# Three of an expert's 24 weight residuals move from VectorE to GpSimd in a two-layer encoder kernel

## The chip, the cores and the metric

The kernel runs on one core of a Trainium2 chip as one launch. The metric is the device time of that launch in microseconds (us), and lower is better. Engines are named as in the profile: PE is TensorE's matmul, PEld its weight load, DVE is VectorE, ACT is ScalarE, POOL is GpSimd, SP is SyncE, whose queue issues the weight loads.

## The reference

Two identical layers work on 512 tokens of width 1024 in float32. Each has a mixer (a state-space scan, a stick-breaking attention and a retention, gated and projected) and a mixture of experts. Only the latter is touched. Every token goes to two of 16 experts, and an expert has three 1024x1024 weights:

```python
def expert_block(args):
    xb, e = args
    hb = jax.nn.silu(xb @ w1[e]) * (xb @ w3[e])
    return hb @ w2[e]
```

The results are weighted by the router's gates and added up for each token.

## The kernel before

**Precision by splitting.** A float32 product is made of three matmuls in fp32r. Each operand is split into a rounded part and the rest: for a weight, ACT copies the raw tile into `wh` (fp32r), and then DVE computes `wl = raw - wh`. `mm3` multiplies with high times high, high times low and low times high. The two lines that matter:

```python
        with self.tc.high_priority(0 if self.calm else self.ahead):
            self.cut = (nc.scalar.copy(hv, v).ins,
                        (eng or nc.vector).tensor_tensor(lv, v, hv.bitcast(F32), OP.subtract).ins)
```

`wh` is line L342 in the profile and `wl` is L343. The argument `eng` of `split_half` chooses the engine of the residual; without it that is DVE.

**The experts.** A weight is loaded as four transfers of 1 MB (`raw`, 128 partitions x 2048), and each transfer holds two k-tiles of 128x1024. So an expert has 24 k-tiles: k = 0 to 7 for each of W1, W3 and W2. For one k-tile PE runs six matmuls of 512 columns (`mm3` for n = 0 and n = 1): L348 with `wh`, L349 with `wl`, L350 with `wh` again. L349 is the first that needs `wl`. The tokens of an expert lie in 96 slots (`CAP`).

**Buffers.** The pool `split` has four `wh` and four `wl`. So ACT can write the `wh` of a k-tile only when PE is through with the k-tile four before it. Raw tiles have some ten buffers of 1 MB in several pools, taken in a fixed order (`ORDER`).

**Order.** The loop over e in `moe` issues W1 of expert e (`expert_in`), then W2 of expert e-1 (`expert_out`), the transposes of the tokens of e+1 (`tx`, with `hx` written by ACT and DVE, L1266 and L1267), the gather of the tokens of e+2 (`fetch`, L1182, an indirect DMA that POOL issues), W3 of e, and then `expert_mid`: `sl = silu(a1) * a3` (ACT L1291, DVE L1292), its transposes (L1264) and their split (`gh`, `gl`, L1266 and L1267). The output `y` of W2 is scaled by the gate on ACT (L1313) and stored from ACT's queue. Each engine runs its own queue in order. A planner writes these queues out at build time, from the priorities given in the code and from costs that it assumes; the splits get a lead of 200 places (`AHEAD`).

**POOL in the experts' stage.** It issues the gathers. In layer 0, from expert 4 (`PREP`) on, it also computes the parameters of layer 1's state-space scan (`s5_params`), in pieces that the generator `step()` lets go, two an expert, until the generator is done and `prep` is None again. In layer 1 there is no next layer, and POOL has the gathers alone. POOL computes the residuals of expert 0's first four k-tiles in either layer, and some of the mixer's.

Of the kernel before, what the change touches and what calls it, by code (L numbers as in the profile page):

```python
# [25 lines left out]
NE = 16  # L26
# [12 lines left out]
PREP = 4  # L39
# [84 lines left out]
class Kernel:  # L124
# [1147 lines left out]
    def expert_in(self, w, x, mkload, tag, ready=()):  # L1272
        ps = [self.bank(t, "e13")[0:CAP] for t in tag]
        for u in range(4):
            if 2 * u >= len(ready):
                v = mkload(w, u)
            for kk in range(2):
                k = 2 * u + kk
                h, lo = ready[k] if k < len(ready) else self.split_half(v[:, kk:kk + 1, :], (1, 1024))
                for n in range(2):  # L1280
                    ns = slice(n * 512, (n + 1) * 512)
                    self.mm3(ps[n], x[0][k], x[1][k], h[:, 0, ns], lo[:, 0, ns], k == 0, k == 7)
        return ps

    def expert_mid(self, pool, a1, a3):
        nc = self.nc
        sl = pool.tile([P, D], F32, tag="sl", name="sl", bufs=1)[0:CAP]
        h, lo = (pool.tile([P, KD * CAP], F32R, tag=n, name=n, bufs=1) for n in ("gh", "gl"))
        for n in range(2):
            ns = slice(n * 512, (n + 1) * 512)  # L1290
            nc.scalar.activation(sl[:, ns], a1[n], AF.Silu)  # L1291
            nc.vector.tensor_tensor(sl[:, ns], sl[:, ns], a3[n], OP.mult)  # L1292
        return self.transpose_split(sl, h, lo)

    def expert_out(self, pool, w, g, mkload, dst, us=range(4), ps=None, y=None, gate=None):
        nc = self.nc
        ps = ps or [self.bank("z", "e2")[0:CAP] for _ in range(2)]
        for u in us:
            v = mkload(w, u)
            for kk in range(2):  # L1300
                k = 2 * u + kk
                h, lo = self.split_half(v[:, kk:kk + 1, :], (1, 1024))
                for n in range(2):
                    ns = slice(n * 512, (n + 1) * 512)
                    self.mm3(ps[n], g[0][k], g[1][k], h[:, 0, ns], lo[:, 0, ns], k == 0, k == 7)
        if dst is None:
            return ps
        if callable(dst):
            return dst(ps)
        y = y or pool.tile([P, D], F32, tag="y", name="y", bufs=1)  # L1310
        for n in range(2):
            ns = slice(n * 512, (n + 1) * 512)
            nc.scalar.activation(y[0:CAP, ns], ps[n], AF.Copy, scale=gate)  # L1313
        nc.scalar.dma_start(dst, y[0:CAP])

    def moe(self, l, lg, nb, rs):
# [6 lines left out]
        with self.pool("mw") as mw, ExitStack() as spare:  # L1323
            self.wx = spare.enter_context(self.pool("wx"))

            def mk(e):
                def load(w, u):
                    key = order.pop(0)
                    order.append(key)
                    return self.load(w[e, u * 256:(u + 1) * 256, :].rearrange("(k p) f -> p k f", p=P), (2, 1024),  # L1330
                                     *slot(key))
                return load
# [7 lines left out]
            ready = []  # L1340
            self.calm = True
            for u in range(2):
                v = mk(0)(W1, u)
# [3 lines left out]
            with tc.high_priority():  # L1347
# [13 lines left out]
                for k in range(KD):  # L1361
                    self.gathered((ps[k][:, 0:256], ps[k][:, 256:]), nxt, k, 2, P)
            pend = prep = None
            y = []

            def step():
                nonlocal prep
                if prep is None:
                    return
                with tc.issue_after(self.fetched):  # L1370
                    done = next(prep, 0) == 0
                if done:
                    prep = spare.close()
                    self.wx = spare.enter_context(self.pool("wx"))
                    order.append("wx")
            for e in range(NE):
                if e == PREP and l + 1 < self.layers:
                    order[:] = [k for k in order if k[1] != "x"]
                if e == 1:
                    with tc.issue_after(self.mid[1]):  # L1380
                        self.places(r, self.hi)
                g = max(i for i, (a, n) in enumerate(GROUPS) if e >= a)
                at = e - GROUPS[g][0]
                if g == 0:
                    x = [[t[k // 4][:, k % 4, at * P:at * P + CAP] for k in range(KD)] for t in nxt]
                else:
                    x = cur
                with ExitStack() as after:
                    if e == 0:
                        after.enter_context(tc.issue_after(r["dv"]))  # L1390
                        after.enter_context(tc.issue_after(r["ex"]))
                    a1 = self.expert_in(W1, x, mk(e), ("pj", "pj"), ready if e == 0 else ())
                self.calm = False
                if e == 0:
                    with tc.issue_after(self.chosen):
                        self.gates(r, self.hi)
                        self.slots(mw, r, 0)
                if e == NE - 1:
                    half = self.expert_out(mw, W2, pend, mk(e - 1), None, range(2))
                elif pend is not None:  # L1400
                    y13 = self.keep.tile([P, D], F32, tag="hx", name="y", bufs=8) if e == NE - 2 else None
                    self.expert_out(mw, W2, pend, mk(e - 1), Y[(e - 1) * CAP:e * CAP, :], y=y13, gate=r["gate"][e - 1])
                step()
                if at == 0 and e < NE - 2:
                    A = self.slots(mw, r, g + 1)
                if 0 < e < NE - 1:
                    cur = self.transpose_split(xr, self.hx(KD * CAP), self.hx(KD * CAP), "zo", False)
                if e < NE - 2:
                    with tc.high_priority():
                        xr = self.fetch(r, e + 2)  # L1410
                if e == NE - 2:
                    self.rest(A, r, mw)
                    self.overflow(l, r, mw, Y, y13[:, 0:T])
                a3 = self.expert_in(W3, x, mk(e), ("b", "b"))
                if e == NE - 1:
                    self.expert_out(mw, W2, pend, mk(e - 1), lambda ps: y.append(self.last_y(ps, 0)), range(2, 4), half)
                pend = self.expert_mid(mw, a1, a3)
                if e == PREP and l + 1 < self.layers:
                    spare.close()
                    sp = spare.enter_context(self.pool("s5p"))  # L1420
                    prep = self.s5_params(sp, self.s5_loads(l + 1), nc.gpsimd, 1)
                step()
# [196 lines left out]
```

## Time and profile before

| what | us |
|---|---|
| median of 3 runs | 2226.86 |
| lowest and highest of them | 2226.26, 2234.1 |
| the profiled execution's own time | 2214.86 |
| its span from first to last instruction | 2213.1 |
| busy in that span: PE, DVE, ACT, POOL | 2114.7, 1545.0, 1230.4, 505.0 |

The experts' stages lie at about 500 to 1085 us (layer 0) and 1590 to 2150 us (layer 1). The profiled execution is 12 us shorter than the median of the timed ones. A row of a timeline gives the start from the span's start, the duration (or that of xN merged instructions), engine, line, operation, what is written and read, and, in brackets, how long the engine had been idle and what it had waited for. Matmuls are pipelined: one of 512 columns starts about 0.23 us after the one before it, though its row shows about 0.39 us.

### The profile page before, as it was taken

What the parts mean: (1) busy time and instruction counts of PE and PEld (TensorE: products, weight loads), DVE (VectorE), ACT (ScalarE), POOL (GpSimd) and SP (SyncE); (2) the same over time, 40 slices, a digit from 0 to 9 for tenths busy, and PEclk for the clock granted to TensorE, in tenths of its full rate; (3) what the DMA queues carried; (4) which work ended last, traced back from release to release, by engine and by line L of the source; (5) the groups of instructions that cost most, each with busy time, mean ns of one, the idle gap of its engine ahead of it and who ended that gap; (6) DMA issues with size and microseconds to landing.
All of it is one profiled execution on the core that took longest, in us unless ns stands there. A gap on an engine that the chain in (4) does not pass through costs nothing. (4 is left out here: it accounts for less than half of the span.)

```text
span 2213.1 us, 27508 instructions
## 1 busy us (share of the span) xinstructions
PE 2114.7 (96%) x10178; PEld 1557.3 (70%) x10181; DVE 1545.0 (70%) x1986; ACT 1230.4 (56%) x1548; POOL 505.0 (23%) x535
## 2 busy tenths in 40 slices
PE   6999999998999999998899999999899999999987
PEld 5668678876777766665666877888767776666664
DVE  8443533459999899887663535434799998888877
ACT  4333123336888777776544331223488887777763
POOL 5410142122039825000260202411410000000004
PEclk9988999999999999999999999999999999999999
DMA  5121275337999999998731213352499999999973
GB/s 192 54 52 53 65 246 194 103 121 280 385 346 375 375 368 340 376 379 315 260 138 45 76 57 124 105 190 96 148 347 386 388 385 352 380 364 380 365 301 130
DMA packets 192461, 533.16 MB, mean 241 GB/s; under 512 B 18545, under 2 KB 72433, under 8 KB 192306
## 3 DMA queue, kind: packets, MB, share of 16 engines
q1 hardware_dynamic: 173312, 476.69, 58.2%
q0 software_dynamic: 8032, 28.84, 3.9%
q10 hardware_dynamic: 10962, 25.67, 3.4%
q8 instruction: 84, 1.38, 0.3%
q14 instruction: 71, 0.58, 0.1%
HBM read 501.14 MB, written 27.00 MB: 239 GB/s over the span
## 5 line engine op out<-in xcount | busy, mean ns | idle before, releaser
L343 DVE TENSOR_TENSOR wl<-raw,wh 128x1024 fp32r<-128x1024 f32 x850 | 1042.3, 1261 | 345.5 <-ACT wh L342 310.6
L342 ACT CAST wh<-raw 128x1024 fp32r<-128x1024 f32 x872 | 896.0, 1050 | 426.7 <-PE e L350 152.8
L349 PE MATMUL e<-wl,hx 128*96 128x512 f32 x1024 | 408.9, 399 | 9.4 <-DVE wl L343 9.4
L350 PE MATMUL e<-wh,hx 128*96 128x512 f32 x1024 | 408.2, 399 | 0.0
L348 PE MATMUL e<-wh,hx 128*96 128x512 f32 x1024 | 383.4, 397 | 10.0 <-PEq L1496 9.9
L348 PE MATMUL pjf<-hx,wh 128*128 128x512 f32 x608 | 244.7, 403 | 4.8 <-DVE v L215 4.8
L350 PE MATMUL pjf<-hx,wl 128*128 128x512 f32 x608 | 244.2, 402 | 2.5 <-DVE wl L343 2.5
L349 PE MATMUL pjf<-hx,wh 128*128 128x512 f32 x608 | 244.6, 402 | 0.8 <-DVE hx L216 0.7
L349 PEld LDWEIGHTS e<-wl,hx 128*96 128x96 f32 x1024 | 167.0, 163 | 86.0 <-DVE wl L343 20.0
L348 PEld LDWEIGHTS e<-wh,hx 128*96 128x96 f32 x1024 | 166.4, 163 | 78.9 <-issue 11.4
L350 PEld LDWEIGHTS e<-wh,hx 128*96 128x96 f32 x1024 | 166.9, 163 | 66.1 <-issue 0.6
L349 PE MATMUL e<-wl,gh 128*96 128x512 f32 x512 | 204.0, 398 | 5.9 <-DVE wl L343 5.4
L350 PE MATMUL e<-wh,gl 128*96 128x512 f32 x512 | 201.2, 394 | 2.6 <-DVE gl L1267 2.6
L1182 POOL DMA_INDIRECT xr<-xd,idx x28 | 46.3, 1655 | 655.8 <-PE tx L1264 523.2
L348 PE MATMUL e<-wh,gh 128*96 128x512 f32 x512 | 180.2, 394 | 0.0
L348 PEld LDWEIGHTS pjf<-hx,wh 128*128 128x128 f32 x608 | 115.9, 191 | 33.4 <-DVE v L215 6.0
L350 PEld LDWEIGHTS pjf<-hx,wl 128*128 128x128 f32 x608 | 115.7, 190 | 29.5 <-DVE wl L343 3.0
L349 PEld LDWEIGHTS pjf<-hx,wh 128*128 128x128 f32 x608 | 115.7, 190 | 29.2 <-DVE hx L216 1.9
L349 PEld LDWEIGHTS e<-wl,gh 128*96 128x96 f32 x512 | 82.6, 161 | 49.8 <-DVE wl L343 18.1
L348 PEld LDWEIGHTS e<-wh,gh 128*96 128x96 f32 x512 | 82.5, 161 | 35.3
L350 PEld LDWEIGHTS e<-wh,gl 128*96 128x96 f32 x512 | 82.5, 161 | 35.2 <-DVE gl L1267 3.5
L956 POOL TENSOR_TENSOR mg<-mg,gsg 128x512 f32<-128x512 f32 x32 | 42.9, 1345 | 211.6 <-DVE gsg L955 187.3
(500 smaller groups left out, 2823.4 us busy)
## 6 DMA issues: line engine op xcount, KB each, us to landing
raw<-in_moe_w_dram SPq DMA_DIRECT2D x384, 1024.0 KB, 7.7
raw<-in_w_in_dram SPq DMA_DIRECT2D x44, 1024.0 KB, 5.3
yd<-y ACTq DMA_DIRECT2D x28, 384.0 KB, 6.0
raw<-in_w_out_dram SPq DMA_DIRECT2D x8, 1024.0 KB, 5.0
yd<-zr ACTq DMA_DIRECT2D x14, 384.0 KB, 5.2
row<-hd POOLq DMA_DIRECT2D x8, 512.0 KB, 7.1
rawu<-in_w_up_c_dram SPq DMA_DIRECT2D x8, 512.0 KB, 3.4
xd<-row POOLq DMA_DIRECT2D x8, 512.0 KB, 3.6
```

The source lines that it names most:

```text
L342: self.cut = (nc.scalar.copy(hv, v).ins, (eng or nc.vector).tensor_tensor(lv, v, hv.bitcast(F32), OP.subtract).ins)
L343: (eng or nc.vector).tensor_tensor(lv, v, hv.bitcast(F32), OP.subtract).ins)
L348: mm(out, lh, rh, start=start, stop=False)
L349: mm(out, lh, rl, start=False, stop=False)
L350: mm(out, ll, rh, start=False, stop=stop)
L956: nc.gpsimd.tensor_tensor(mg[m], mg[m], sg, OP.add)
L1182: self.fetched = self.nc.gpsimd.indirect_dma_start(out=t, out_offset=None, in_=self.x_dram[:, :], in_offset=at).ins
```

## The change

The fifth k-tile (k = 4) of W1, W3 and W2 gets its `wl` from POOL in place of DVE, where a flag allows it. The flag `free` is set for expert e when e is 2 to 14, no `s5_params` is under way, and e is neither 4 nor 5. In iteration e this concerns W1 and W3 of expert e and W2 of expert e-1. Nothing else changes; `wh`, the matmuls, buffers and loads stay.

```diff
-                h, lo = ready[k] if k < len(ready) else self.split_half(v[:, kk:kk + 1, :], (1, 1024))
+                h, lo = ready[k] if k < len(ready) else self.split_half(v[:, kk:kk + 1, :], (1, 1024), self.helper(k))
...
+    def helper(self, k):
+        return self.nc.gpsimd if self.free and k == 4 else None
...
-                h, lo = self.split_half(v[:, kk:kk + 1, :], (1, 1024))
+                h, lo = self.split_half(v[:, kk:kk + 1, :], (1, 1024), self.helper(k))
...
             pend = prep = None
+            self.free = False
...
+                self.free = 2 <= e < NE - 1 and prep is None and (e < PREP or e > PREP + 1)
```

## Rows read from the trace of the kernel before

**Rows 1.** Windows, early and late experts of layer 1: stretch, length, PE, PEld, DVE, ACT, POOL busy, PEclk, DMA share, GB/s.
```profile
1691.00:1795.00 104.00, 104.00 (x492) 73.53 (x491) 96.50 (x95) 85.51 (x96) 3.98 (x3) 1.00 1.01 388
1903.00:2047.00 144.00, 140.79 (x649) 97.79 (x648) 123.07 (x124) 111.40 (x129) 5.49 (x4) 1.00 0.95 372
```

**Rows 2.** Waits in 1650 to 2100 us, of PE and of ACT: total, times, longest.
```profile
PE e L349 <- DVE wl L343: 5.1, 13, 0.5
...
ACT y L1313 <- PE e L350: 9.8, 8, 1.3
...
ACT wh L342 <- DMA raw<-in_moe_w_dram: 0.8, 2, 0.4
```

**Rows 3.** Timeline of ACT, layer 1: outputs y of two early experts, then two late ones.
```profile
1720.61 0.68 ACT L1313 ACTIVATE y<-e,gate 96x512 f32<-96x512 f32 x1
...
1755.27 0.68 ACT L1313 ACTIVATE y<-e,gate 96x512 f32<-96x512 f32 x1
...
1897.01 1.26 ACT L1313 ACTIVATE y<-e,gate 96x512 f32<-96x512 f32 x2 [1.25 <-PE e L350]
...
1933.01 1.26 ACT L1313 ACTIVATE y<-e,gate 96x512 f32<-96x512 f32 x2 [1.26 <-PE e L350]
```

**Rows 4.** Timeline, early expert, W1, k = 4: its wl, and PE's first use.
```profile
1769.88 1.23 DVE L343 TENSOR_TENSOR wl<-raw,wh 128x1024 fp32r<-128x1024 f32 x1
...
1772.98 0.40 PE L349 MATMUL e<-wl,hx 128*96 128x512 f32 x1
```

**Rows 5.** Timeline, an early expert: DVE's sl and the transposes that wait for it.
```profile
1737.78 0.68 DVE L1292 TENSOR_TENSOR sl<-sl,e 96x512 f32<-96x512 f32 x1
...
1738.61 0.52 PE L1264 MATMUL tx<-cs,sl 96*128 96x96 f32 x4
```

**Rows 6.** Source line L343 on POOL, whole span: duration min, median, max in ns.
```profile
L343 POOL TENSOR_TENSOR wl<-raw,wh x22: 2332/2367/3599, 16.9 to 1592.9; 128x1024 fp32r<-128x1024 f32 x22
```

**Rows 7.** Timeline, late expert, W3: wl of k = 3, wl of k = 4, PE's first use of k = 4.
```profile
1936.94 1.22 DVE L343 TENSOR_TENSOR wl<-raw,wh 128x1024 fp32r<-128x1024 f32 x1
...
1938.07 1.22 DVE L343 TENSOR_TENSOR wl<-raw,wh 128x1024 fp32r<-128x1024 f32 x1
...
1939.70 0.40 PE L349 MATMUL e<-wl,hx 128*96 128x512 f32 x1
```

**Rows 8.** Timeline, late expert, W1, k = 4: its wl, and PE's first use.
```profile
1949.87 1.23 DVE L343 TENSOR_TENSOR wl<-raw,wh 128x1024 fp32r<-128x1024 f32 x1 [0.95 <-ACT wh L342]
...
1951.72 0.45 PE L349 MATMUL e<-wl,hx 128*96 128x512 f32 x1
```

**Rows 9.** Timeline, late expert, W2: wl of k = 3, PE's first use of k = 4.
```profile
1961.20 1.22 DVE L343 TENSOR_TENSOR wl<-raw,wh 128x1024 fp32r<-128x1024 f32 x1
...
1964.19 0.39 PE L349 MATMUL e<-wl,gh 128*96 128x512 f32 x1
```

**Rows 10.** Timeline, late expert, W2: a gather on POOL, and PE's first use of k = 4.
```profile
1997.55 1.73 POOL L1182 DMA_INDIRECT xr<-xd,idx  x1 [37.95 <-PE tx L1264]
...
2000.26 0.39 PE L349 MATMUL e<-wl,gh 128*96 128x512 f32 x1
```

**Rows 11.** Timeline of DVE and POOL ahead of layer 1's experts.
```profile
1580.85 0.22 DVE L1058 SCALAR_TENSOR_TENSOR lg<-lg,ve,rc 128x16 f32<-128x16 f32 x1
...
1583.16 4.65 POOL L343 TENSOR_TENSOR wl<-raw,wh 128x1024 fp32r<-128x1024 f32 x2
...
1583.35 2.19 DVE L1058 SCALAR_TENSOR_TENSOR lg<-lg,ve,rc 128x16 f32<-128x16 f32 x1
```

**Rows 12.** Groups on DVE in 877 to 887 us (POOL busy with s5_params), then in 951 to 961 us (POOL idle).
```profile
L343 DVE TENSOR_TENSOR wl<-raw,wh 128x1024 fp32r<-128x1024 f32 x7 | 10.6, 1573 | 0.3 <-ACT wh L342 0.3
...
L343 DVE TENSOR_TENSOR wl<-raw,wh 128x1024 fp32r<-128x1024 f32 x8 | 9.2, 1220 | 0.3 <-ACT wh L342 0.3
```

**Rows 13.** Timeline, early expert (e = 2), W3: a gather on POOL, and PE's first use of k = 4.
```profile
1691.94 2.16 POOL L1182 DMA_INDIRECT xr<-xd,idx  x1 [32.68 <-PE tx L1264]
...
1692.67 0.39 PE L349 MATMUL e<-wl,hx 128*96 128x512 f32 x1
```

## The prediction

> **What bounds the kernel now.** I first read the windows, to see which engine an experts' stage leaves no idle time, and the waits, to see what PE waits for. In the early experts PE is busy for the whole of 104 us, in the late ones for 140.79 of 144, at a granted clock of 1.00 [rows 1]. In 450 us of layer 1's experts PE waits for one thing only, the `wl` of a k-tile on DVE: 13 waits, 5.1 us in all [rows 2]. ACT waits 0.8 us for weight loads there [rows 2], so loads are not the bound, though the DMA engines are 0.95 busy [rows 1]. DVE is busy for 0.93 of the early and 0.85 of the late stretch [rows 1]. So PE sets the time, and DVE matters only where a `wl` comes too late for it.
>
> Then I read the timelines, because the margin differs. An early expert takes 34.66 us from one output `y` to the next, a late one 36.00 [rows 3]. In the late ones `y` stands in ACT's queue ahead of the `wh` of the next W3 tiles and waits 1.26 us for PE there, as it does in 8 experts [rows 2, 3]. What is behind it comes late, and for some tiles PE and DVE run almost without a margin.
>
> The reader is to see the margin in three places. Early, the `wl` of k = 4 ends at 1769.88 + 1.23 = 1771.11, and PE takes it at 1772.98: 1.87 us to spare [rows 4]. Late, in W3, it ends at 1939.29 and is taken at 1939.70: 0.41 [rows 7]. Late, in W1, it is 1951.72 - 1951.10 = 0.62 [rows 8]. In W2 it is about the same.
>
> **How many.** In layer 1 the flag holds for e = 2 to 14, 13 experts. In layer 0 it holds for 2 and 3, and again when `s5_params` is done. The generator has 15 pauses and gets one step in expert 4 and two in each after it, so the 16th and last step falls in expert 12, after the flag was set: 13 and 14 follow. That makes 17 experts, 51 instructions.
>
> **What one moved residual costs.** On DVE it is 1.22 us [rows 12], on POOL 2.37 in the median, 2.33 at least and 3.60 at most [rows 6]. So the result comes 1.15 us later even if POOL starts at once. Where the margin is 1.87 this is hidden by it; where it is 0.41 or 0.62 it isn't.
>
> POOL may have to wait, too, and DVE behind it. A 128x16 instruction on DVE takes 0.22 us alone and 2.19 us beside one of POOL's residuals [rows 11]. While POOL ran the state-space parameters, the `wl` on DVE took 1573 ns in the mean, and 1220 without them [rows 12]. I take it that a `wl` on either engine waits until the other's is done. DVE then loses 2.37 us and is spared 1.22 each time, and wins back some 0.25 us on each later tile (PE takes 1.38 us for one, six starts 0.23 apart, while DVE's back to back take 1.14: eight in 9.2 us [rows 12]). So the seven tiles in between suffice.
>
> The Trainium skill, page "SBUF — State Buffer", section "Who interferes with whom", has this as an exclusive lock: a VectorE instruction with two SBUF inputs and a GpSimd instruction that reads SBUF block one another for the whole instruction. The trace agrees, with 2.19 us for 0.22 [rows 11]. With that rule the sum is the 24 us below; without it W3 and W2 could start up to 1.2 us earlier, and the sum would be about 14.
>
> **The sum, late experts.** PE's stall is POOL's end less the time at which PE takes the tile now, with 0.05 us for the handover.
> - W3: DVE is at k = 3 until 1938.16, POOL then ends at 1940.53, and PE takes the tile at 1939.70 [rows 7]: 0.85. Seven experts of layer 1 and one of layer 0 look like this: 6.8 us.
> - W1: POOL starts when DVE does now, at 1949.87, and ends at 1952.24 against 1951.72 [rows 8]: 0.57. Eight and two: 5.7 us.
> - W2: DVE is at k = 3 until 1962.42, POOL ends at 1964.79 against 1964.19 [rows 9]: 0.65. Four and one: 3.2 us.
> - W2 in three more experts of layer 1: POOL is at a gather until 1999.28, then ends at 2001.65 against 2000.26 [rows 10]: 1.4 each, 4.2 us.
>
> That is 19.9 us. Nothing takes it back: ACT's `y`, `gh` and `hx` wait for PE and move with it, and the loads have no wait to give.
>
> **The sum, early experts.** The tiles themselves are hidden by the 1.87 us. But DVE's `sl` stands behind the k = 5 tile in two experts of layer 1, and its end, 1738.46, is only 0.15 us ahead of the transposes that need it [rows 5]. POOL delays it by about 1.05 us, so 0.9 each, 1.8 us. In the five other early experts `sl` stands elsewhere; I take 0 to 0.9 each, 2 in sum. Together 4 us.
>
> **What is gained.** DVE gets 51 x 1.22 = 62 us less work, but PE's waits for it are what that can shorten: 5.1 us in layer 1 [rows 2], and these come from a late `wh` behind `y`, not from DVE's load. I take nothing. The raw buffers come free no later: their second residual (k = 5) ends after POOL's in any case. A gather behind a residual on POOL is 2.4 us later, and what it brings is used an expert later.
>
> So +24 us: 2214.86 to 2238.9 for the profiled execution. The timed runs lie higher, with a median of 2226.86, and I add the same: **2251 us**, 1.1% slower. The bounds of the price: +14 if the engines don't hinder one another (24 less W3's 6.8 and W2's 3.2, whose residuals could then start up to a whole `wl` earlier), and, if each W1 and early residual waits out one more `wl` of DVE (3.60 for 2.37), up to +36. This case has 2240 to 2263.
>
> **The rivals.**
> - *Hidden.* The planner orders the queues so that k = 4 keeps a margin of 1.2 us or more in late experts too, or what is lost there is partly won by DVE's relief. For it: early experts have the margin [rows 4]. Against it: `y`, not DVE, opens the gap [rows 3]. 0 to +10 us: 2227 to 2237. The Trainium skill, page "Perfetto Trace Analysis", section "Optimizing Scalar/DVE Operations", says that moving work off a saturated DVE may help, but between DVE and GpSimd might not; here the most that it could give is the 5.1 us of rows 2 and about 1 in layer 0.
> - *Faster.* The planner, with less work on DVE, writes the late experts' ACT queue as the early ones': `y` between `wh` tiles and not ahead of them. That gives 36.00 - 34.66 = 1.34 us for each of 16 experts [rows 3], 21 us, less 0.6 for each of 17 as early ones: 11 us net, 2216; with the early price near nothing, 2206. It decides from nearly all of the late experts. Against it: PE and ACT get no other work, and the residual's engine touches neither `y` nor `wh`.
> - *POOL's queue stands.* A gather waits for PE's transposes, and the residual of W3 stands behind it. At e = 2 the gather starts at 1691.94, the residual would end at 1691.94 + 2.16 + 2.37 = 1696.47, and PE takes it at 1692.67 [rows 13]: 3.8 us. If half of the 17 experts have it, 9 x 3.8 = 34 on top: 2285. Against it: DVE has this residual ahead of the transposes there now, so POOL's queue may have it ahead of the gather.
> - *The flag holds rarely.* Were it only layer 1's 13, the sum falls by some 4 us; this is in the first case's range.
>
> **How the numbers follow.** My forecast has a chance of 0.50, *hidden* 0.27, *POOL's queue* 0.12, *faster* 0.11. About 0.5%, 11 us, is what a measurement can tell from no change: below 2216 is faster, above 2238 slower. So faster 0.11, same 0.27, slower 0.62. The range leaves out the fastest (under 2218) and the far end of the standing queue (over 2275), some 0.2 together: 2218 to 2275.
>
> **What would show it.** Right: 51 more `wl` on POOL of 2.3 to 3.6 us and 51 fewer on DVE; PE's waits for `wl` on POOL near 20 us, most of them 0.5 to 1.5 us long, in late experts; DVE's longest `wl` over 2 us; a late expert near 38 us from `y` to `y`. Wrong, if PE's waits stay at 5 us in layer 1, if a DVE `wl` beside POOL's keeps its 1.22 us, if the place of `y` in ACT's queue changes, or if POOL's residuals stand behind waiting gathers.

## The result, and the profile after

The changed kernel takes 2238.07 us in the median of 20 runs (2234.75 to 2251.18), the kernel before 2222.4 in 20 runs beside it (2206.15 to 2234.1). The ratio is 1.0098, with a 95% interval of 1.0081 to 1.0115: about 1% slower. (It is not the quotient of the two medians, which is 1.0071.) The forecast was 2251 us, 1.1% slower, in a range of 2218 to 2275. The profiled execution has a span of 2233.8 us, 20.7 more than the 2213.1 of before, where the forecast had 24.

First the groups of line L343, the residuals, on DVE and POOL, in the profile after (count, busy us, mean ns, idle time before them):
```profile
L343 DVE TENSOR_TENSOR wl<-raw,wh 128x1024 fp32r<-128x1024 f32 x805 | 1041.3, 1331 | 372.0 <-ACT wh L342 366.8
...
L343 POOL TENSOR_TENSOR wl<-raw,wh 128x1024 fp32r<-128x1024 f32 x67 | 165.8, 2479 | 605.8 <-ACT wh L342 605.8
```
POOL had 22 residuals [rows 6] and has 67, so 45 were moved, and not 51. On DVE the same group had 850 before:
```profile
L343 DVE TENSOR_TENSOR wl<-raw,wh 128x1024 fp32r<-128x1024 f32 x850 | 1042.3, 1261 | 345.5 <-ACT wh L342 310.6
```
45 residuals of 1.22 us are 55 us. DVE's busy time fell by 1.0 us: the instructions moved, but DVE is busy as long as before.

PE's waits after, in 1650 to 2100 us, the stretch of [rows 2]:
```profile
PE e L349 <- POOL wl L343: 12.2, 20, 0.8
PE e L349 <- DVE wl L343: 5.0, 13, 0.5
```
The old waits for DVE stand as they were (5.1 us, 13 times). New are 20 waits for POOL.

The outputs `y` of two late experts after, which answer to the second pair of [rows 3]:
```profile
1942.19 1.26 ACT L1316 ACTIVATE y<-e,gate 96x512 f32<-96x512 f32 x2 [1.26 <-PE e L350]
...
1980.61 1.26 ACT L1316 ACTIVATE y<-e,gate 96x512 f32<-96x512 f32 x2 [1.26 <-PE e L350]
```
From `y` to `y` it is 38.42 us instead of 36.00, and `y` waits for PE as before. The 2.4 us lie in the three tiles with k = 4 and the one or two behind each. Here is W3's, in the timeline after: DVE's k = 3, POOL's k = 4, DVE's k = 5, and PE's first use of k = 4:
```profile
1946.12 1.22 DVE L343 TENSOR_TENSOR wl<-raw,wh 128x1024 fp32r<-128x1024 f32 x1
...
1946.92 2.67 POOL L343 TENSOR_TENSOR wl<-raw,wh 128x1024 fp32r<-128x1024 f32 x1 [9.69 <-ACT wh L342]
...
1947.83 2.85 DVE L343 TENSOR_TENSOR wl<-raw,wh 128x1024 fp32r<-128x1024 f32 x1 [0.49 <-ACT wh L342]
...
1949.64 0.47 PE L349 MATMUL e<-wl,hx 128*96 128x512 f32 x1 [0.61 <-POOL wl L343]
```
POOL takes 2.67 us beside DVE's k = 3 and ends at 1949.59; PE starts 0.05 later, which is the handover. DVE's k = 5 starts at 1947.83, while POOL is at work, and takes 2.85 us instead of 1.22: it ends 1.09 us after POOL. W1 is alike, with a POOL that need not wait for DVE (2.40 us) and a DVE that does (2.57 for k = 5):
```profile
1959.94 2.40 POOL L343 TENSOR_TENSOR wl<-raw,wh 128x1024 fp32r<-128x1024 f32 x1 [10.36 <-ACT wh L342]
1962.49 1.71 POOL L1182 DMA_INDIRECT xr<-xd,idx  x1
...
1960.85 2.57 DVE L343 TENSOR_TENSOR wl<-raw,wh 128x1024 fp32r<-128x1024 f32 x1 [1.24 <-ACT wh L342]
...
1962.39 0.48 PE L349 MATMUL e<-wl,hx 128*96 128x512 f32 x1 [0.75 <-POOL wl L343]
```
The gather (L1182) now stands behind the residual in POOL's queue, not ahead of it.

One loss has nothing to do with a residual's length. In layer 0, expert 4, ACT issues small loads for the next mixer (`small`, L472 the last of them). After, then before:
```profile
640.58 6.99 ACTq L472 DMA_DIRECT2D small<-in_small_dram  x1
```
```profile
647.33 2.21 ACTq L472 DMA_DIRECT2D small<-in_small_dram  x1
```
ACT's queue stands for 6.99 us instead of 2.21, and no `wh` is made in that time. PE waits 3.1 us for one of them, and then runs behind a late ACT. Waits of PE, 600 to 700 us, after:
```profile
PE e L348 <- ACT wh L342: 3.1, 1, 3.1
```

**Where the 20.7 us are.** For each k-tile I took the start of PE's first use of its `wl`, counted from the layer's first such use, and subtracted the same of the kernel before. The table has this shift in us at some tiles n (24 an expert; late experts begin near n = 156 in layer 1), and the timed ratio.

| run | layer 0: n = 84 | 100 | end | layer 1: 84 | 156 | 336 | end | ratio (95% interval) |
|---|---|---|---|---|---|---|---|---|
| changed kernel | -0.08 | 6.48 | 10.06 | -0.06 | -0.07 | 19.04 | 18.26 | 1.0098 (1.0081 to 1.0115) |
| e1_k1 | 3.31 | 7.90 | 8.71 | 2.70 | 3.24 | 5.22 | 3.95 | 1.0055 (1.0032 to 1.0077) |
| e2_late | 0.20 | 0.20 | 5.02 | -0.05 | -0.08 | 18.75 | 18.37 | 1.0058 (1.0036 to 1.0079) |
| e3_early | 0.34 | 6.04 | 7.21 | 0.03 | 0.02 | 0.03 | -0.62 | 1.0007 (0.9987 to 1.0027) |
| e4_half | 0.94 | 6.95 | 7.24 | 0.87 | 0.84 | 4.77 | 4.47 | 1.0028 (1.0007 to 1.0050) |
| e5_y_later | 0.17 | 2.59 | -1.85 | -0.11 | -0.28 | -6.81 | -6.61 | 0.9918 (0.9889 to 0.9948) |
| e6_gather_first | -0.02 | 6.64 | 10.32 | -0.08 | -0.09 | 18.98 | 18.29 | 1.0128 (1.0096 to 1.0160) |
| e7_move_and_y | 0.36 | 5.70 | 4.90 | -0.03 | -0.23 | 12.65 | 15.34 | 1.0076 (1.0049 to 1.0103) |
| e8_pool_beside | 5.15 | 11.68 | 19.48 | 4.54 | 6.42 | 46.14 | 46.21 | 1.0277 (1.0246 to 1.0307) |
| e9_small_on_sp | -0.08 | -0.06 | 4.48 | 0.04 | -0.01 | 19.02 | 18.40 | 1.0089 (1.0057 to 1.0121) |
| e10_y_split | 1.03 | 1.10 | 6.15 | 0.80 | 2.11 | 3.93 | 4.26 | 0.9999 (0.9975 to 1.0022) |
| e11_y_split_sp | 1.32 | 1.82 | 8.23 | 0.97 | 2.30 | 4.15 | 3.34 | 1.0038 (1.0013 to 1.0063) |
| e12_k7 | 0.74 | 6.77 | 8.02 | 0.57 | 1.19 | 3.25 | 2.09 | 1.0033 (1.0007 to 1.0058) |

For the changed kernel: 10.06 + 18.26 = 28.3 us in the experts, less 7.7 because its first layer's experts happened to begin earlier (first use of `wl` at 507.8 against 515.5), is 20.6, the span's 20.7. That earlier start is no gain of the change: nothing ahead of the experts was touched. The first 500 us, after and then before (PE, PEld, DVE, ACT, POOL busy, PEclk, DMA share, GB/s):
```profile
0.00:500.00 500.00, 465.85 (x2354) 367.00 (x2357) 249.12 (x449) 162.46 (x256) 137.07 (x186) 0.97 0.37 122
```
```profile
0.00:500.00 500.00, 470.77 (x2336) 368.78 (x2339) 242.44 (x427) 158.91 (x251) 132.20 (x184) 0.95 0.37 119
```
The granted clock was 0.97 in the one and 0.95 in the other. The 13 profiled executions other than before's begin the experts of layer 0 between 507 and 517 us, and the mixer of layer 1 takes between 489 and 498. So a span is uncertain by some 8 us from each, while the shifts inside an experts' stage repeat to some 0.1 us: layer 1's end at 18.26, 18.37, 18.29 and 18.40 in four kernels with the same late residuals. I judge the experiments by the shifts, and by the timed ratio where the whole matters.

The two differ, and always the same way. In all 13 kernels the timed ratio gives less than the end shifts of both layers together, by 0.2 to 10.6 us, 5 in the mean. For the changed kernel it gives 21.8 us (18.0 to 25.6) where the shifts give 28.3. Every shift is counted against one profiled execution of the kernel before, which took 2214.86 us where the timed median is 2222.4. That its experts ran some 5 us shorter than usual would explain the difference, but there is no second trace of that kernel, and this isn't shown.

### The profile page after: what moved, and what is told of

Its sections match the earlier page's. It is cut to its first block, busy times and chain, and to the rows that moved or that the text cites. A ratio compares the mean times of both kernels' runs of the same rounds, so it can differ in the third digit from the quotient of the medians.

```text
span 2233.8 us, 27532 instructions
## 1 busy us (share of the span) xinstructions
PE 2113.8 (95%) x10178; PEld 1551.4 (69%) x10181; DVE 1546.1 (69%) x1941; ACT 1230.6 (55%) x1548; POOL 604.4 (27%) x580
## 3 DMA queue, kind: packets, MB, share of 16 engines
q8 instruction: 84, 1.38, 0.3%
## 5 line engine op out<-in xcount | busy, mean ns | idle before, releaser
L343 DVE TENSOR_TENSOR wl<-raw,wh 128x1024 fp32r<-128x1024 f32 x805 | 1041.3, 1331 | 372.0 <-ACT wh L342 366.8
L343 POOL TENSOR_TENSOR wl<-raw,wh 128x1024 fp32r<-128x1024 f32 x67 | 165.8, 2479 | 605.8 <-ACT wh L342 605.8
L1182 POOL DMA_INDIRECT xr<-xd,idx x28 | 48.9, 1746 | 218.5 <-PE tx L1264 148.6
```

The lines of the kernel that those rows point to most:

```text
L1182: self.fetched = self.nc.gpsimd.indirect_dma_start(out=t, out_offset=None, in_=self.x_dram[:, :], in_offset=at).ins
```

## The experiments

The theory: a moved residual costs its lateness minus the slack of its tile (the prediction's margin: from the end of its `wl` to PE's first use of it; at 0.05 us, the handover, PE waits), and what DVE loses to POOL's access takes away the gain on DVE. Rivals are named in each expectation. The first four runs change which residuals move.

**e1_k1**, another tile:
```
-        return self.nc.gpsimd if self.free and k == 4 else None
+        return self.nc.gpsimd if self.free and k == 1 else None
```


> As the change, but the tile moved to POOL is k = 1 of each matrix in place of k = 4: as many residuals on POOL, in the same experts. Margin theory (a residual on POOL ends 2.4 us after its wh, and costs PE only what exceeds the tile's margin, which only late experts lack): in late experts the margin of k = 1 is 1.9 us in W3, and in W1 two sl instructions, which DVE can run beside POOL, stand behind it, so both are hidden; in W2 DVE is at k = 0 until 1957.69, POOL ends at 1960.1 and PE wants it at 1959.31, 0.8 us in each of about 9 late experts: +7 us or +0.3%. Port theory (POOL's hold of the second read costs DVE, and so PE, the same wherever it stands): as the change, +22 us or +1.0%.

Measured: by n = 336 layer 1's late experts lose 5.22 - 3.24 = 2.0 us, and 19 with k = 4, at the same number of residuals. So a residual's length on POOL alone doesn't set the price. PE takes W2's k = 1 0.68 us later (a step of 2.13 us instead of 1.45), but k = 2, where PE waited for a late `wh` anyway, follows after 1.70 instead of 2.02, and k = 3 after 1.39 instead of 1.47: most of the loss goes into a wait that was there. In the early experts k = 1 does cost, 3.3 and 2.7 us by n = 84, where the margin theory had both hidden and k = 4 cost nothing. Most of it is one tile in each layer (2.4 us), where a small instruction of DVE waits for POOL's residual, and `sl`, which PE waits for, stands behind it:
```profile
1675.67 2.36 DVE L1234 TENSOR_TENSOR pos<-pf,off 128x8 int32<-128x8 f32 x1
...
1679.14 0.55 PE L1264 MATMUL tx<-cs,sl 96*128 96x96 f32 x4 [1.84 <-DVE sl L1295]
```
The same instruction took 0.16 us before. With 4.6 us of layer 0's other loss (n = 84 to 100) the whole is +0.55%, between the two theories' +0.3 and +1.0.

**e2_late** and **e3_early** split the 45 by experts (the first added line is e2_late, the second e3_early):
```
-                self.free = 2 <= e < NE - 1 and prep is None and (e < PREP or e > PREP + 1)
+                self.free = 7 <= e < NE - 1 and prep is None
+                self.free = 2 <= e < 7 and prep is None and (e < PREP or e > PREP + 1)
```


> The change in late experts alone: the flag is set for e = 7 to 14, so in layer 1 for eight experts and in layer 0 for 13 and 14, 30 of the change's 45 residuals. Margin theory: layer 1 loses 18 to 19 us and layer 0 3.5, as in the changed kernel, +22 us or +1.0%; the single 6.5 us stall of layer 0 behind a slow DMA issue on ACT is not there if it belongs to the early residuals. Port theory: two thirds of the change's cost, +15 us or +0.7%.

> The change in early experts alone: e = 2 and 3 in both layers, 6 in layer 1, 15 residuals. Margin theory: no PE wait for a residual on POOL, 0 us, and same as before; if the single 6.5 us stall of layer 0 comes from the early residuals, it is here, +6.5 us or +0.3%. Port theory: a third of the change's cost, +7 us or +0.3%, as many short waits.

Measured: the late ones alone give all of layer 1's loss (18.37 of 18.26) and 5.0 us in layer 0. The early ones alone give nothing in layer 1 (0.03 at n = 336). But they bring the loss at layer 0's tile 96 (5.7 us), which e2_late lacks. So the two losses are separate: the late residuals cost about 22 to 23 us, and moving layer 0's experts 2 and 3 disturbs ACT's loads.

**e4_half**, only columns 512 to 1023 of each moved residual on POOL, the rest on DVE:
```
...
+            if two:
+                nc.gpsimd.tensor_tensor(lv[:, :, 512:], v[:, :, 512:], hv[:, :, 512:].bitcast(F32), OP.subtract)
+                lv, v, hs = lv[:, :, 0:512], v[:, :, 0:512], hv[:, :, 0:512]
...
```


> The change with half of each residual on POOL (columns 512 to 1023), the other half on DVE. Margin theory: POOL takes 1.2 us and DVE 0.6, one after the other, so the residual ends about 1.8 us after its wh at the latest; W3 exceeds its margin by 0.3 us, W1 and W2 by 0.05 at most: +3 us or +0.15%. Port theory: half of the hold, half of the cost, +11 us or +0.5%.

Measured: layer 1 ends 4.5 us late instead of 18.3. POOL's half takes 1.80 us in the median, so the result still comes later than DVE's 1.22. W3 loses 0.3 us and most of the other tiles nothing, as expected; the three W2 with the least slack (0.16 us) lose 0.5 to 0.7:
```profile
L344 POOL TENSOR_TENSOR wl<-raw,wh x45: 1261/1797/2148, 571.4 to 2125.0; 128x512 fp32r<-128x512 f32 x45
```

**e8_pool_beside** separates POOL's access from POOL's lateness: DVE keeps all residuals, and POOL computes the 45 a second time, for nobody.
```
...
+    def beside(self, k, v, h):
+        if k == 4:
+            with self.tc.high_priority(0 if self.calm else self.ahead):
+                d = self.split.tile([P, 1024], BF16, tag="dm", name="dm", bufs=1)
+                self.nc.gpsimd.tensor_tensor(d, v, h[:, 0].bitcast(F32), OP.subtract)
...
```


> The kernel before, all residuals on DVE; POOL computes the 45 residuals of k=4 a second time into a tile of its own (half the bytes out) that nobody reads. Theory 'shared access': DVE's residuals beside POOL's take 2.2 to 2.9 us instead of 1.2, PE waits for DVE's wl of k=4 and k=5 in late experts, and layer 1 loses 6 to 15 us. Rival 'POOL's latency alone': DVE's residuals keep 1.2 to 1.4 us there and layer 1 loses under 2 us.

Measured: the sign was right and the size far off. Layer 1 loses 46 us, where 6 to 15 were expected, and more than the move itself. POOL's instruction, and DVE's beside it, in a late W3 of this run:
```profile
1945.26 2.62 POOL L1290 TENSOR_TENSOR dm<-raw,wh 128x1024 bf16<-128x1024 f32 x1 [9.44 <-ACT wh L342]
```
```profile
1945.55 3.42 DVE L343 TENSOR_TENSOR wl<-raw,wh 128x1024 fp32r<-128x1024 f32 x1
```
DVE starts 0.29 us after POOL and ends 1.09 after POOL's end, at 1948.97: it did its work only when POOL was through. PE takes this tile 1.85 us later, the 2.20 that DVE lost less the slack. In W3 `wl` of k = 4 itself is held here, with a slack of 0.4 us; in W1 it is k = 5, which loses 1.5. In the changed kernel k = 5 is held alone, and DVE comes to it sooner because it has no k = 4 to do. The Trainium skill, page "SBUF — State Buffer", section "Who interferes with whom", says that a VectorE instruction with two SBUF inputs contends with a GpSimd instruction that reads SBUF, under an exclusive lock, and that the order of issue decides which of the two blocks; the trace agrees, with 3.42 us for 1.22 on DVE, which came second.

The other runs change the slack, or the place of layer 0's loss.

**e5_y_later**, on the kernel before: ACT evicts `y` behind `wh` of W3's k = 3 and not ahead of k = 2.
```
...
+                if k == 3 and self.late:
+                    put, self.late = self.late, None
+                    with self.tc.issue_after(self.cut[0]):
+                        put()
...
```
(`late` is the two evictions and the store at the end of `expert_out`.)

> The kernel before (no residual moved), but ACT puts the eviction of y behind wh of the W3 tile k=3 instead of between the last matmul of W2 and the first tiles of W3. Theory 'margin': late experts are tight because y stands ahead of wh on ACT; then the period of a late expert falls from 36.00 us towards the 34.66 us of an early one, PE's waits for DVE's wl in 1650:2100 (5.1 us, 13 times) fall under 2 us, and the whole is 5 to 12 us faster. Rival 'loads': the late experts are tight because the raw tiles land late; then period and waits stay and the time is within 3 us of before.

Measured: 2203.52 us in the median against 2218.98, and a ratio of 0.9918: 0.82% faster than before, and so faster than both kernels. The shifts of its experts are 8.5 us of the timed 18.2 (11.5 to 24.6); where the rest lies isn't shown. In 1650 to 2100 us PE's waits for `wl` fall from 5.1 us to 0.7, and `y` no longer waits for PE:
```profile
PE e L350 <- DVE wl L344: 0.7, 4, 0.2
```
```profile
1895.90 1.25 ACT L1325 ACTIVATE y<-e,gate 96x512 f32<-96x512 f32 x2
1930.86 1.25 ACT L1325 ACTIVATE y<-e,gate 96x512 f32<-96x512 f32 x2
```
A late expert takes 34.96 us, near the early ones' 34.66 [rows 3]. The place of `y` did open the gap, and this, not DVE's load, is what the waits of [rows 2] could give.

**e7_move_and_y**, both changes together.

> All 45 residuals on POOL as in the changed kernel, and y's eviction put later as in the run that only does that. Theory 'margin': the price of a moved residual is its lateness minus the slack of its tile; with y out of the way the W3 tiles k=4 of late experts (0.85 us each) get over 1 us of slack and cost nothing, W1 (1.05 with what follows) less than half, so that layer 1's loss falls from 18.3 us to under 8 us and the whole is within 10 us of before. Rival 'POOL is slow': a residual of 2.4 to 2.7 us instead of 1.2 costs 0.6 to 1.4 us wherever the expert is, and layer 1's loss stays over 14 us.

Measured: at n = 336 layer 1 is 12.65 us late; against e5_y_later, which has the same `y`, the move costs 12.65 + 6.81 = 19.5 us, as much as before. By its end alone the rival is right. The slack was less than I had taken, though. `y` now stands ahead of k = 4's `wh`, and in e5_y_later W3's k = 4 has 0.82 us (0.40 before), W1's 0.81 (0.63), W2's only 0.16 (0.63). W3's price falls from 0.77 us at k = 4 to 0.45, as the rule says: POOL ends 2.47 us after `wh`, DVE 1.25 after it, and 1.22 less 0.82 is 0.40. W1 keeps its 0.7, because `wh` of that tile comes 0.23 us later here than in e5_y_later: that leaves a slack of 0.58, and 1.22 less 0.58 is 0.64. W2's share rises, by 0.37 at k = 2 among others. So slack was moved about, not made. Why layer 1 loses 2.7 us more after n = 336 here was not followed up.

**e12_k7** moves 30 residuals where slack is: k = 7 of W2 and W3.
```
-        return self.nc.gpsimd if self.free and k == 4 else None
+        return self.nc.gpsimd if self.free and k == 7 else None
```
(and no helper for W1.)

> The changed kernel with 30 residuals on POOL: k=7 of W2 and W3 (not W1) in the same 15 experts instead of k=4 of all three. Theory 'slack': POOL ends a residual 2.75 us after wh; wh of these tiles is 3.1 to 3.4 us ahead of PE in late experts, and the next tile of DVE has 1.6 us of slack for the 1.6 us that POOL's access holds it; so layer 1 loses under 3 us (k=4 of W2 and W3: 0.63 and 0.85 us an expert, some 12 us for eight). Rival 'every residual on POOL costs the same': layer 1 loses 10 us or more.

Measured: layer 1's late experts lose 3.25 - 1.19 = 2.1 us in all. The same two tiles of an expert cost about 1.5 us with k = 4, some 12 in eight late experts. POOL's residual uses up the slack and little more (it ends a median of 0.05 us ahead of PE, where DVE had 1.15 to 1.38), and the next tile has the slack for DVE's delay. With e1_k1 this decides for slack, against one price for every residual. Still nothing is gained: the early experts lose 1.2 us, and layer 0 has its other loss (ACT's issue takes 7.64 us).

**e6_gather_first** and **e9_small_on_sp** are on layer 0's loss. In the first, W2's k = 4 in iteration 3 of layer 0 stays on DVE, behind which a gather waits on POOL. (By the loop's order this is the W2 of expert 2, not of expert 3 as the expectation has it.) In the second, SP and not ACT issues the small loads, all but the first (the last two lines):
```
+                self.first3 = l + 1 < self.layers and e == 3
-                h, lo = self.split_half(v[:, kk:kk + 1, :], (1, 1024), self.helper(k))
+                h, lo = self.split_half(v[:, kk:kk + 1, :], (1, 1024), None if self.first3 else self.helper(k))
-                    prep = self.s5_params(sp, self.s5_loads(l + 1), nc.gpsimd, 1)
+                    prep = self.s5_params(sp, self.s5_loads(l + 1, nc.sync), nc.gpsimd, 1)
```


> The changed kernel, with one residual fewer on POOL: that of W2 k=4 of layer 0's expert 3, behind which the row gather of POOL waited; 44 remain. Theory 'gather into the loads': the late gather pushes the small parameter loads on ACT's queue into the stream of weight loads, and the last of them holds ACT for 7.0 us; then its issue falls back to about 2.2 us, PE's wait for ACT's wh (3.1 us) goes, and layer 0's shift at its 96th tile falls from +6.5 us to under 0.5 us: 6 us faster than the changed kernel. Rival 'any move in layer 0': ACT's order is another in that expert and the 7 us issue stays, time that of the changed kernel (about +20 us on before).

> The changed kernel with all 45 residuals on POOL; but the second mixer's small parameter loads (all but the first) are issued by SP, not by ACT. Theory 'ACT held': the 6.5 us that layer 0 loses at its 96th tile are ACT's issue of the last small load (7.0 us); on SP it holds no wh, layer 0's shift there falls under 1 us, layer 1's 18.3 us stay, and the time is 5 to 7 us under the changed kernel. Rival 'loads late anyway': SP is held as long, its weight loads come later, PE waits for ACT's wh behind raw instead, and layer 0 still loses 5 us or more at that place.

Measured: e6 didn't do what was expected. ACT's issue takes 7.12 us there, and layer 0 loses 6.64. That excludes the gather behind this residual, which now starts 33.3 us ahead of ACT's issue instead of 21.5. The next one, behind W3's residual, starts 9.6 us ahead of it in both kernels, and e6 says nothing of it. In e9 the shift at n = 100 is -0.06 us and layer 1 as in the changed kernel: in the profiled executions the 6.5 us are ACT's issue. (SP issues these loads 45 us later, and its last two issues take 2.0 and 3.4 us there without a loss to PE.) In the timed runs this loss isn't shown: e9's ratio (1.0089) can't be told from the changed kernel's, and e3_early, whose shifts sum to 6.6 us, nearly all of it this loss, was timed at +1.6 (-2.9 to +6.0). Why the issue takes so long stays open. The rows show only what goes with it. The two 64 KB loads issued ahead of it land 14.3 and 13.1 us after their issue, and 6.8 and 5.7 before. After, then before (KB each, us to landing):
```profile
small<-in_c_dram ACTq DMA_DIRECT2D x1, 64.0 KB, 14.3
s5c<-in_c_dram ACTq DMA_DIRECT2D x1, 64.0 KB, 13.1
```
```profile
small<-in_c_dram ACTq DMA_DIRECT2D x1, 64.0 KB, 6.8
s5c<-in_c_dram ACTq DMA_DIRECT2D x1, 64.0 KB, 5.7
```
The issue takes 6.3 to 8.3 us in all eight kernels in which POOL computes residuals of layer 0's early experts and ACT issues the load. Of those without, it takes 2.2 in the kernel before and in e2_late, 0.34 in e10_y_split and 5.08 in e5_y_later. So a long issue needs no residual on POOL. In the first eight the last gather starts 5.1 to 11.6 us ahead of the issue, in the other four 13.6 to 14.7. That this gather is the cause isn't shown; no run moved it alone.

**e10_y_split** and **e11_y_split_sp** try to better e5_y_later: y's halves behind k = 3 and k = 6, and in e11 the small loads on SP too.
```
...
+                if k in (3, 6) and self.late:
+                    with self.tc.issue_after(self.cut[0]):
+                        self.late(k == 6)
+                    self.late = self.late if k == 3 else None
...
```


> The kernel before, no residual moved; y's two halves are evicted apart, behind wh of W3 k=3 and of k=6, where the earlier run put both behind k=3. If slack builds up at 0.25 us a tile and a half costs 0.63 us, the dip at k=4 (slack 0.82 us after the earlier run) becomes about 1.4 us, and the layer 1 shift at its 336th tile goes from -6.8 us to between -7 and -11: 0.3% or less faster than with both halves at k=3. Rival: the wait left in late experts is that of W2 k=2 (slack 0.06 us in both), which y does not touch; then the time is that of the earlier run, -0.8%.

> As the run with y's halves apart, and the second mixer's small loads issued by SP. If ACT's issue of the last small load is what holds layer 0 by 2.6 us at its 96th tile when y is late (its issue took 5.1 us there), this gives about 2.5 us on top, some -1.0% in all; if SP is held instead, nothing or a loss.

Measured: both missed. W3 gets its slack (1.98 us at k = 4), but W1's k = 0 in the next expert now comes 3.13 us after the tile ahead of it instead of 1.62, with its `wh` ready 4.4 us early: DVE's `wl` is late there, at a slack of 0.05. In DVE's queue `sl`, which waits 2.77 us for PE's last matmul of W3, now stands ahead of it:
```profile
1908.58 1.28 DVE L1297 TENSOR_TENSOR sl<-sl,e 96x512 f32<-96x512 f32 x2 [2.77 <-PE e L351]
1909.78 4.62 DVE L344 TENSOR_TENSOR wl<-raw,wh 128x1024 fp32r<-128x1024 f32 x4
```
Before, and in e5_y_later, `wl` of W1's k = 0 and k = 1 are ahead of that `sl`. So the planner, given another place for `y`, changed DVE's order too. The gain of e5_y_later is gone: 0.9999 (0.9975 to 1.0022), and 1.0038 in e11.

## Why the prediction was right, and where it wasn't

**Late experts, 19.9 us: right, 22.4 measured.** This sums what the eight tiles of a matrix lose. W3: eight times 0.84 to 0.88 us, 6.8, as forecast (8 x 0.85; with its 0.05 for the handover the forecast's own working gives 0.88). W1: ten, of which nine lose 0.95 to 0.99 and one 0.55, 9.2 for 5.7. This term was undersized: the 0.57 was the tile k = 4 alone (0.64 measured), and DVE's k = 5, held by POOL, and k = 6 lose another 0.3. The forecast had DVE win this back unseen. W2: five of 0.61 to 0.64, 3.1 for 3.2.

**The gather's term, 4.2 us: size near, reason wrong.** The three W2 matrices lose 0.99 to 1.11 us, 3.2 in all, but POOL isn't at a gather there; the gather goes behind the residual of W1. They cost more than the other W2 because DVE had an `hx` of the transposes to do just ahead of k = 4 before, which left this tile a slack of only 0.16 us. As the gather goes behind, the rival *POOL's queue stands* didn't come either.

**Early experts, 4 us: wrong.** Layer 1 has 0.16. The 1.87 us of slack [rows 4] hid the tiles, as forecast; the delay of `sl` was priced for two experts, 4 and 5, whose W1 residuals aren't moved at all. That is also the miscount: the flag shuts out e = 4 and 5 in both layers, not only where `s5_params` runs, so 15 experts and not 17 have it. Where `sl` does meet a moved residual it isn't held: one runs in its 0.68 us at 1668.60, inside POOL's residual of 1667.85 to 1670.25.

**Not foreseen: 6.5 us of ACT's issue** in layer 0. The prediction looked at POOL's queue for what the move displaces, not at ACT's. How much of it the timed difference holds is open, as said above.

**The gain, nothing: right.** PE's old waits stand at 5.0 us, and DVE's busy time fell by 1.0 of 55 us, for in late experts a `wl` beside POOL's takes 2.6 to 2.9 us. One sign came out smaller than forecast: PE's waits for `wl` on POOL are 16.0 us in 26 waits over the whole run, not near 20. The Trainium skill, page "Perfetto Trace Analysis", section "Optimizing Scalar/DVE Operations", warns that moving work between these two might not help; this trace agrees, with 1041.3 us for 1042.3. So the exclusive access is right, and *hidden*, 0 to +10 us, was wrong for k = 4 in late experts; for k = 1 and k = 7 it would have been near.

The experts lost 28.3 us where 24 were forecast: 24, and 2.5 more in late experts, and 6.5 not foreseen, less the early 4 that didn't come and 0.7 that layer 1 wins back in its last experts. So the misses cancel in part, and that the sum came so near is partly luck. The timed difference is 15.7 us by the medians (2238.07 - 2222.4) and 21.8 (18.0 to 25.6) by the ratio: the forecast's 24 lies inside that interval, and the 28.3 of the shifts does not.

## What to carry to other kernels

Taking work off an engine that isn't the bound gains nothing by itself. Ask which tile's result comes too late and what stands ahead of it: here it was `y` in ACT's queue, and moving it was worth 0.8%. Price a moved instruction tile by tile, its new end less the time of its use, and put it where the slack is (for W2 and W3 of eight late experts k = 7 cost 2 us and k = 4 some 12). Then read the queues again, for the planner may order them anew, as in e10_y_split. And where two engines share an access, count the moved instruction's time on both.

## What the runs showed that I had not expected

- DVE's busy time hardly moves when 45 residuals leave it (1042.3 to 1041.3 us): POOL's 2.4 us of access come back on DVE as 1.4 to 1.6 us of waiting in the next `wl` of late experts.
- A useless residual on POOL beside a needed one on DVE costs 46 us in one layer, more than twice the move (18.3).
- Issuing one small load (31 KB) holds ACT's queue for 0.3 us in one kernel, 2.2 in two and 5.1 to 8.3 in nine others, and the `wh` behind it with it.
- A DVE instruction of 0.16 us (`pos`, two inputs in SBUF) takes 2.36 us beside a residual on POOL, while `sl`, which reads `e`, the matmuls' sums, beside its own tile, keeps its 0.68.
